# Decoder block on one core: sums of squares from a token-major input, phase tables made once and copied, GpSimd's wide work on VectorE

## The chip, the core and the metric

The kernel runs on one core of a Trainium2 chip. The core has five engines with a queue of instructions each, which run in order and meet by semaphores: TensorE (PE, matmuls; its weight loads are shown as PEld), VectorE (DVE), ScalarE (ACT), GpSimd (POOL) and SyncE (SP), which here only issues DMAs. The metric is the device time of one execution in microseconds. The comparison is with the median of three runs of the kernel before.

## What is computed

The reference is one decoder block on x of 1024 tokens by 1024 channels, in float32. After a normalization by the mean square of each token, one projection gives q, k, v, a gate and u. Retention of four heads takes q, k, v; a diagonal state-space model (S5) with 32 groups of 16 channels and 64 complex states takes u. Both results go through w_out, and a squared-ReLU MLP follows.

```python
h = rmsnorm(x, norm_mix_pre[i])                  # x * rsqrt(mean(x*x) + eps) * gain
q, k, v, gate, u = split(h @ w_in[i])
y_ret = silu(gate) * groupnorm(retention(rope(q), rope(k) * d**-0.5, v))
# S5: states s[l] = lam_bar * s[l-1] + b_bar u[l];  y = Re(c s) + d u
y_ssm = gelu(s5_scan(u, ...));  a, b = split(y_ssm @ w_glu[i]);  y_ssm = a * sigmoid(b)
x = x + rmsnorm(concat(y_ret, y_ssm) @ w_out[i])
h = rmsnorm(x, norm_mlp_pre[i])
x = x + rmsnorm(square(relu(h @ w_ff1[i])) @ w_ff2[i])
```

## The kernel before

Every float32 matmul operand is split in a high and a low part (split, ACT makes hi, DVE makes lo), and a product is three matmuls of 128x512 (mm3). Channels lie on the partitions; a tile is mostly 128x512, half of the tokens (hf 0 or 1). The order of instructions on each engine is made by the tile framework, which schedules with a timeline simulation; the code gives a sequence and a few extra dependences (load with a lead, in_place).

The front, up to the first matmul of w_out (tile mx), is what the change touches.

- x_half (L183) loads one of 16 halves of x, splits it, squares it in place on ACT (L190) and adds the square to xacc on POOL (L191). norm_sums turns xacc to sums per token with small matmuls (tile ns_x), rstd (L216) takes the power -1/2 on POOL (L220), norm_bcast spreads the result over the partitions with matmuls (tile nb_x), and ACT copies it to R (L277).
- The u product (L264 to L282) takes four PSUM banks for each half, u_0 and u_1. ACT evicts them to us (L273), DVE multiplies by R to uT (L280), and SP writes uT to DRAM (ud), from which the S5 parts read it back in another layout (UT).
- Between these, DVE makes the tables of S5: powers pw, qw, and vw, and the phase factors fa (16 steps) and fb (8 steps), by doubling (double_up, cmul).
- ssm_part runs for eight parts of four groups. outer makes W and VV (DVE, with one product, tmp, on POOL at L453); W gives kps and the Toeplitz tile MR (memset on POOL, eight DMAs), wps and WT. cmul at L490 makes the part's phase tables Fr and Fi, Fr on DVE and Fi on POOL (L310 to L312). xps = WT x UT; A and B are xps turned by Fr and Fi (L494 to L497, the last on POOL); a scan on DVE (L500); the turn back to SS (L503 on POOL, L505 to L509 on DVE); yps takes MR and SS; ACT applies the Gelu to Y, SP writes it to DRAM (yd), from which it comes back as ysT for the glu product.
- ssm() makes the parts run one behind the other, and tick() (L632) takes one step of them for each half of a gate or q/k projection (gate_unit, tile pg; qk_unit, tile pj), and two steps at every fourth tick. v_pair (tile v) comes after eight units. qk_unit applies rope on DVE and adds on POOL (L661). head_half is the retention; it multiplies q by xis on POOL (L600).
- After the projections come glu (tile gl), w_out (mx) and the MLP (f1, f2).

All loads and copies go through load (L114), on SP's queue. cmul (L306) writes one complex product as six operations, the first three on one engine and the last three on another, here V and GP for the phase tables:

```python
def cmul(e1, e2, o_r, o_i, ar, ai, br, bi, tr, ti):
    e1.tensor_tensor(o_r, ar, br, op=MUL)     # L307
    e1.tensor_tensor(tr, ai, bi, op=MUL)
    e1.tensor_tensor(o_r, o_r, tr, op=SUB)
    e2.tensor_tensor(o_i, ar, bi, op=MUL)     # L310
    e2.tensor_tensor(ti, ai, br, op=MUL)
    e2.tensor_tensor(o_i, o_i, ti, op=ADD)
```

Of the kernel before, what the change touches and what calls it, by code (L numbers as in the profile page):

```python
# [24 lines left out]
P = 128  # L25
D = 1024
L = 1024
KB = D // P
T = 8
NCH = L // P  # L30
H = 4
G = 32
# [18 lines left out]
def hybrid_block_kernel(ctx, tc, x, gain, wu, wv, wqkg, wglu, wout, wff1, wff2, lam, bc, dsk,  # L51
# [129 lines left out]
    hT, wus, xacc = [], [], [half("xacc0"), half("xacc1")]  # L181

    def x_half(k, hf):  # L183
        xr = half(f"x_{k}{hf}")
        load(xr, x[k][:, hs[hf]])
        r = split_new(f"h{k}{hf}", xr, g_pre[:, k:k + 1])
        if k == 0:
            S.activation(xacc[hf], xr, AF.Square)
        else:
            S.activation(xr, xr, AF.Square)  # L190
            GP.tensor_tensor(xacc[hf], xacc[hf], xr, op=ADD)  # L191
        return r

    for k in range(KB):
# [3 lines left out]
        hT.append([h0])  # L198
    for k in range(KB):
        hT[k].append(x_half(k, 1))  # L200
    lm = const("lm", [P, 3, G])
    load(lm, lam)
    sg_ = const("sgn_t", [P, 2])
    load(sg_, sgn)
    s_pm, s_mp = sg_[:, 0:1], sg_[:, 1:2]
# [8 lines left out]

# [49 lines left out]
    for hf in range(2):  # L264
# [9 lines left out]
        rr = norm_sums(f"x{hf}", [xacc[hf]], 4)  # L274
# [107 lines left out]
    def double_up(r, i, j, w, n):  # L382

        sh = [P, n, G]
        cmul(V, V, r[:, w:w + n], i[:, w:w + n], r[:, 0:n], i[:, 0:n],
             r[:, w - 1:w].to_broadcast(sh), i[:, w - 1:w].to_broadcast(sh),
             t8[:, 0, 0:n], t8[:, 1, 0:n])
# [17 lines left out]
    fa_r, fa_i = half("fa_r", shape=(P, 16, G)), half("fa_i", shape=(P, 16, G))  # L405
    fb = half("fb", shape=(P, 2, T, G))
# [5 lines left out]
    tt(fa_r[:, 0], t0, t1, MUL)  # L412
    tt(t0, sn, t1, MUL)
    ts(fa_i[:, 0], t0, s_mp, MUL)
    for w in (1, 2, 4, 8):
        double_up(fa_r, fa_i, 1, w, w)
# [3 lines left out]
    V.tensor_copy(fbr[:, 1], fa_r[:, 15])  # L420
    V.tensor_copy(fbi[:, 1], fa_i[:, 15])
    for w, n in ((1, 1), (2, 2), (4, 2)):
        double_up(fbr[:, 1:], fbi[:, 1:], 1, w, n)
    double_up(fbr[:, 1:], fbi[:, 1:], 1, 6, 1)
# [9 lines left out]

    def ssm_part(ei):
        g0 = ei * 4
# [6 lines left out]
        def outer(dst, a, lr, b, li, nm):  # L443
# [9 lines left out]
            GP.tensor_tensor(tmp, bx(b), by(li), op=MUL)  # L453
# [23 lines left out]
        Fr, Fi = half(f"Fr{ei}", shape=s3), half(f"Fi{ei}", shape=s3)  # L477
        A, B = half(f"A{ei}", shape=s3), half(f"B{ei}", shape=s3)
        shf = [P, 4, T, 16]

        def lowp(m):
            return m[:, :, gs].rearrange("p a g -> p g a").unsqueeze(2).to_broadcast(shf)

        def highp(m):
# [748 lines left out]
```

## Time and profile before

| | |
|---|---|
| time, median of 3 runs | 1126.47 us (1126.09 to 1129.38) |
| the profiled execution | 1127.15 us, span 1125.4 us |
| PE busy | 1065.6 us (95%) |
| DVE busy | 808.4 us (72%), 1433 instructions |
| ACT busy | 487.6 us (43%) |
| POOL busy | 218.9 us (19%), 149 instructions |
| first mx matmul | 401.81 us after the span's start |

Busy shares are means over the whole span. The page also cuts the span in 40 slices of 28 us and gives for each engine a digit, the busy tenths of the slice; so a stretch in which an engine is full stands out. Times in the rows below are from the start of the span. A duration of an instruction reaches from its start to its end with its latency; instructions of one engine overlap a little, so the distance from start to start is what one costs in a full queue.

### The profile page before, as it was taken

The numbers are of one execution on the slowest core, as the hardware profiler recorded it, in microseconds if no ns is written. First come the engines' busy times: TensorE is split into PE (matmuls) and PEld (weight loads), VectorE is DVE, ScalarE is ACT, GpSimd is POOL, SyncE is SP. The second block draws the span as 40 slices with busy tenths as digits, with TensorE's granted clock in tenths as the row PEclk, the third lists the DMA queues.
The fourth block names the chain that finished last, engine by engine and source line by source line (L and its number), as shares of the span: only waits on it lengthen the run. The fifth ranks groups of instructions, "written<-read, shape, count | busy, mean of one in ns | idle before, by whom it ended". The sixth has DMA issues, their size and how long they took to land.

```text
span 1125.4 us, 15280 instructions
## 1 busy us (share of the span) xinstructions
PE 1065.6 (95%) x5264; PEld 903.5 (80%) x5264; DVE 808.4 (72%) x1433; ACT 487.6 (43%) x900; POOL 218.9 (19%) x149
## 2 busy tenths in 40 slices
PE   7789796799999999999999999999999999999995
PEld 6577675698898888878888888888888888888895
DVE  7998989949654610657887788888575786675965
ACT  6411222332554522446665554456462445434712
POOL 4556676526311202230000000000000000000002
PEclk9898898899999999999999999999999999999998
DMA  8223122221123020438637667656793465569424
GB/s 297 79 53 104 49 82 87 60 72 62 34 95 103 20 75 1 168 127 306 222 116 240 225 224 235 231 195 228 281 371 99 156 207 184 171 225 349 137 69 156
DMA packets 122061, 174.24 MB, mean 155 GB/s; under 512 B 34944, under 2 KB 43136, under 8 KB 121984
## 3 DMA queue, kind: packets, MB, share of 16 engines
q1 hardware_dynamic: 121440, 172.75, 45.9%
q8 instruction: 41, 0.67, 0.2%
q10 hardware_dynamic: 544, 0.52, 0.1%
q14 instruction: 36, 0.29, 0.1%
HBM read 126.43 MB, written 45.61 MB: 153 GB/s over the span
## 4 chain that ended last, share of the span: by engine, by line
PE 78%; DVE 12%; issue 3%; SPq 2%; POOL 1%; DMA 1%; ACT 0%; DVEq 0%; ACTq 0%; POOLq 0%
PE f2x L106 15%; PE f2y L106 12%; PE f1z L106 8%; PE f1y L106 8%; PE mx L106 8%; PE f1x L106 7%; PE pj L106 4%; PE v L106 4%; PE gl L106 4%; PE f1w L106 4%; SPq L115 2%; DVE small L298 1%; DVE lo_wqkg L136 1%; DVE B L500 1%; DVE Fr L307 1%
## 5 line engine op out<-in xcount | busy, mean ns | idle before, releaser
L220 POOL TENSOR_TENSOR small<-small 128x4 f32<-128x4 f32 (+1 forms) x9 | 10.2, 1131 | 627.8 <-DVE small L218 627.8
L106 PE MATMUL f2x<-hi_tc,lo_sb 128*128 128x512 f32 x216 | 84.0, 389 | 0.0
L106 PE MATMUL f2x<-lo_tc,hi_sb 128*128 128x512 f32 x216 | 84.0, 389 | 0.0
L106 PE MATMUL f2x<-hi_tc,hi_sb 128*128 128x512 f32 x216 | 83.7, 390 | 0.0
L135 ACT ACTIVATE hi_sa<-rawa 128x512 fp32r<-128x512 f32 x80 | 48.3, 622 | 61.5 <-DVE rawa L799 57.2
L106 PE MATMUL f2y<-hi_tc,hi_sb 128*128 128x512 f32 x192 | 74.7, 389 | 0.0
L106 PE MATMUL f2y<-lo_tc,hi_sb 128*128 128x512 f32 x192 | 74.7, 389 | 0.0
L106 PE MATMUL f2y<-hi_tc,lo_sb 128*128 128x512 f32 x192 | 74.7, 389 | 0.0
L136 DVE TENSOR_TENSOR lo_sa<-rawa,hi_sa 128x512 fp32r<-128x512 f32 x80 | 56.1, 707 | 9.5 <-ACT hi_sa L135 9.5
L106 PE MATMUL pj<-hi_h,hi_wqkg 128*128 128x512 f32 x128 | 51.5, 402 | 0.0
L106 PE MATMUL pj<-lo_h,hi_wqkg 128*128 128x512 f32 x128 | 51.2, 400 | 0.0
L106 PE MATMUL pj<-hi_h,lo_wqkg 128*128 128x512 f32 x128 | 51.0, 399 | 0.0
L106 PE MATMUL f1x<-lo_tb,hi_sa 128*128 128x512 f32 x128 | 50.0, 390 | 0.3 <-DVE lo_tb L136 0.3
L106 PE MATMUL f1x<-hi_tb,hi_sa 128*128 128x512 f32 x128 | 50.1, 392 | 0.0
L106 PE MATMUL f1y<-hi_tb,hi_sa 128*128 128x512 f32 x128 | 49.8, 389 | 0.0
L106 PE MATMUL f1y<-lo_tb,hi_sa 128*128 128x512 f32 x128 | 49.8, 389 | 0.0
L106 PE MATMUL f1y<-hi_tb,lo_sa 128*128 128x512 f32 x128 | 49.8, 389 | 0.0
L106 PE MATMUL f1z<-hi_tb,hi_sa 128*128 128x512 f32 x128 | 49.8, 389 | 0.0
L106 PE MATMUL f1z<-lo_tb,hi_sa 128*128 128x512 f32 x128 | 49.8, 389 | 0.0
L106 PE MATMUL f1z<-hi_tb,lo_sa 128*128 128x512 f32 x128 | 49.8, 389 | 0.0
L106 PE MATMUL f1x<-hi_tb,lo_sa 128*128 128x512 f32 x128 | 49.3, 390 | 0.0
L106 PEld LDWEIGHTS f2x<-hi_tc,lo_sb 128*128 128x128 f32 x216 | 40.6, 188 | 8.5
(401 smaller groups left out, 3207.2 us busy)
## 6 DMA issues: line engine op xcount, KB each, us to landing
rawa<-wff_dram SPq DMA_DIRECT2D x92, 256.0 KB, 3.2
tinx<-td SPq DMA_DIRECT2D x48, 256.0 KB, 3.9
tiny<-td SPq DMA_DIRECT2D x48, 256.0 KB, 3.4
raw_wqkg<-wqkg_dram SPq DMA_DIRECT2D x24, 256.0 KB, 2.8
x<-x_dram SPq DMA_DIRECT2D x16, 256.0 KB, 5.1
raw_wo<-wout_dram SPq DMA_DIRECT2D x16, 256.0 KB, 4.1
xr<-x_dram SPq DMA_DIRECT2D x16, 256.0 KB, 4.1
xs<-mxs SPq DMA_DIRECT2D x16, 256.0 KB, 4.3
```

Source lines behind the costliest of these rows:

```text
L106: r = TE.matmul(out_, lhsT, rhs, **kw)
L115: r = nc.sync.dma_start(dst, src)
L135: after_mark(S.activation(hi, src, AF.Copy))
L136: V.tensor_tensor(lo, src, hi.bitcast(F32), op=SUB)
L220: GP.tensor_tensor(r, t, mhalf[:, 0:n], op=ALU.pow)
L298: V.scalar_tensor_tensor(o, a, s, b, op0=op0, op1=op1)
L307: e1.tensor_tensor(o_r, ar, br, op=MUL)
L500: V.tensor_tensor_scan(B[:, g], rho[:, g0 + g:g0 + g + 1].to_broadcast([P, P]), A[:, g], 0.0, op0=MUL, op1=ADD)
```

## The change

- The squares for the norm no longer come from the halves of x. A second copy of the input, xrow, with tokens on the partitions, is loaded in 16 pieces of 128x512 (x_sums), and ACT squares each with a running sum into a column of xsum. DVE adds two columns (new L278). xacc, its POOL additions and the ns_x matmuls are gone.
- fa and fb are half as wide: the partitions 0 to 63 hold the even parts' groups, 64 to 127 the odd ones'. They are doubled on POOL instead of DVE.
- phase_tables makes Fr and Fi for two parts in one pass (all six operations on DVE). Three DMAs for each of them spread them: the upper half to both halves of the odd part's tile, the lower half to the upper half of the even part's.
- The sign that the tables carried between halves is now in two scalar_tensor_tensor operations (new L525, L535).
- Every other wide operation of POOL in the front goes to DVE: tmp, A (twice), ra/rb, xis, rope.
- tick() takes one step each time.

```diff
@@ -178,31 +178,35 @@
     make_identity(nc, ident)
 
 
-    hT, wus, xacc = [], [], [half("xacc0"), half("xacc1")]
+    hT, wus = [], []
+    xsum = const("xsum", [P, 2, NCH])
 
     def x_half(k, hf):
         xr = half(f"x_{k}{hf}")
         load(xr, x[k][:, hs[hf]])
-        r = split_new(f"h{k}{hf}", xr, g_pre[:, k:k + 1])
-        if k == 0:
-            S.activation(xacc[hf], xr, AF.Square)
-        else:
-            S.activation(xr, xr, AF.Square)
-            GP.tensor_tensor(xacc[hf], xacc[hf], xr, op=ADD)
-        return r
-
+        return split_new(f"h{k}{hf}", xr, g_pre[:, k:k + 1])
+
+    def x_sums(hf):
+        for c in range(4 * hf, 4 * hf + 4):
+            for i in range(2):
+                xt = half(f"xt{c}{i}")
+                load(xt, xrow[c][:, hs[i]])
+                S.activation(xt, xt, AF.Square, accum_out=xsum[:, i, c:c + 1])
+
+    lm = const("lm", [P, 3, G])
+    load(lm, lam)
+    sg_ = const("sgn_t", [P, 2])
+    load(sg_, sgn)
+    s_pm, s_mp = sg_[:, 0:1], sg_[:, 1:2]
     for k in range(KB):
         h0 = x_half(k, 0)
         if k % 2 == 0:
             wus += wload(f"wu{k}", wu[k // 2])
         hT.append([h0])
+    x_sums(0)
     for k in range(KB):
         hT[k].append(x_half(k, 1))
-    lm = const("lm", [P, 3, G])
-    load(lm, lam)
-    sg_ = const("sgn_t", [P, 2])
-    load(sg_, sgn)
-    s_pm, s_mp = sg_[:, 0:1], sg_[:, 1:2]
+    x_sums(1)
     ed = const("ed", [GC, GC])
     load(ed, edge)
     dk = const("dk", [GC, G])
@@ -271,7 +274,9 @@
         us = [half(f"us_{hf}{b}") for b in range(4)]
         for b in range(4):
             S.activation(us[b], pss[b], AF.Copy)
-        rr = norm_sums(f"x{hf}", [xacc[hf]], 4)
+        sums = xsum[:, 0, 4 * hf:4 * hf + 4]
+        V.tensor_tensor(sums, sums, xsum[:, 1, 4 * hf:4 * hf + 4], op=ADD)
+        rr = rstd(f"x{hf}", sums, 4)
         rv.append(rr)
         R.append(half(f"R{hf}"))
         S.activation(R[hf], norm_bcast(f"x{hf}", rr, 4), AF.Copy)
@@ -379,12 +384,13 @@
     tt(t1, t1, t2, SUB)
     tt(ki, t1, t0, MUL)
 
-    def double_up(r, i, j, w, n):
-
-        sh = [P, n, G]
-        cmul(V, V, r[:, w:w + n], i[:, w:w + n], r[:, 0:n], i[:, 0:n],
+    def double_up(r, i, j, w, n, e=V):
+
+        sh = [P, n, r.shape[2]]
+        c = r.shape[2]
+        cmul(e, e, r[:, w:w + n], i[:, w:w + n], r[:, 0:n], i[:, 0:n],
              r[:, w - 1:w].to_broadcast(sh), i[:, w - 1:w].to_broadcast(sh),
-             t8[:, 0, 0:n], t8[:, 1, 0:n])
+             t8[:, 0, 0:n, 0:c], t8[:, 1, 0:n, 0:c])
 
     for w in (1, 2, 4):
         double_up(pr, pi, 1, w, w)
@@ -402,26 +408,33 @@
     ts(rho, e, 1.0, ADD)
 
 
-    fa_r, fa_i = half("fa_r", shape=(P, 16, G)), half("fa_i", shape=(P, 16, G))
-    fb = half("fb", shape=(P, 2, T, G))
+    G2 = G // 2
+    fa = half("fa", shape=(P, 2, 16, G2))
+    fa_r, fa_i = fa[:, 0], fa[:, 1]
+    fb = half("fb", shape=(P, 2, T, G))[:, :, :, 0:G2]
     ts(t0, cm, 1.0, ADD)
     tt(t1, t0, t0, MUL)
     tt(t2, sn, sn, MUL)
     tt(t1, t1, t2, ADD)
     ts(t1, t1, -0.5, MUL, 1.5, ADD)
-    tt(fa_r[:, 0], t0, t1, MUL)
-    tt(t0, sn, t1, MUL)
-    ts(fa_i[:, 0], t0, s_mp, MUL)
+    for i in range(2):
+        ph = slice(64 * i, 64 * i + 64)
+
+        def of_half(m):
+            return m[ph].rearrange("p (j i g) -> p j i g", i=2, g=4)[:, :, i]
+
+        for o, z in ((fa_r, t0), (fa_i, sn)):
+            tt(o[ph, 0].rearrange("p (j g) -> p j g", g=4), of_half(z), of_half(t1), MUL)
     for w in (1, 2, 4, 8):
-        double_up(fa_r, fa_i, 1, w, w)
+        double_up(fa_r, fa_i, 1, w, w, GP)
     fbr, fbi = fb[:, 0], fb[:, 1]
     V.memset(fbr[:, 0], 1.0)
     V.memset(fbi[:, 0], 0.0)
-    V.tensor_copy(fbr[:, 1], fa_r[:, 15])
-    V.tensor_copy(fbi[:, 1], fa_i[:, 15])
+    GP.tensor_scalar(fbr[:, 1], fa_r[:, 15], 1.0, None, op0=MUL)
+    GP.tensor_scalar(fbi[:, 1], fa_i[:, 15], 1.0, None, op0=MUL)
     for w, n in ((1, 1), (2, 2), (4, 2)):
-        double_up(fbr[:, 1:], fbi[:, 1:], 1, w, n)
-    double_up(fbr[:, 1:], fbi[:, 1:], 1, 6, 1)
+        double_up(fbr[:, 1:], fbi[:, 1:], 1, w, n, GP)
+    double_up(fbr[:, 1:], fbi[:, 1:], 1, 6, 1, GP)
     cs = half("cs", shape=(P, G, GC))
     ts(cs, a_c, s_pm, MUL)
     de = half("de", shape=(P, G, GC))
@@ -432,7 +445,35 @@
     s3 = (P, 4, P)
     s4 = (P, 4, T, GC)
 
+    phases = {}
+
+    def phase_tables(j):
+
+        gs = slice(4 * j, 4 * j + 4)
+        shf = [P, 4, T, 16]
+
+        def lowp(m):
+            return m[:, :, gs].rearrange("p a g -> p g a").unsqueeze(2).to_broadcast(shf)
+
+        def highp(m):
+            return m[:, :, gs].rearrange("p a g -> p g a").unsqueeze(3).to_broadcast(shf)
+
+        def v4(m):
+            return m.rearrange("p g (b a) -> p g b a", a=16)
+
+        even, odd = ([half(f"F{z}{2 * j + i}", shape=s3) for z in "ri"] for i in range(2))
+        tr, ti = half(f"ftr{j}", shape=s3), half(f"fti{j}", shape=s3)
+        cmul(V, V, v4(even[0]), v4(even[1]), lowp(fa_r), lowp(fa_i), highp(fbr), highp(fbi),
+             v4(tr), v4(ti))
+        for e, o in zip(even, odd):
+            load(o[0:64], e[64:128])
+            load(o[64:128], e[64:128])
+            load(e[64:128], e[0:64])
+        phases[2 * j], phases[2 * j + 1] = even, odd
+
     def ssm_part(ei):
+        if ei % 2 == 0:
+            phase_tables(ei // 2)
         g0 = ei * 4
         gs = slice(g0, g0 + 4)
         UT = half(f"UT{ei}", shape=s3)
@@ -450,7 +491,7 @@
             V.tensor_tensor(dst, bx(a), by(lr), op=MUL)
-            GP.tensor_tensor(tmp, bx(b), by(li), op=MUL)
+            V.tensor_tensor(tmp, bx(b), by(li), op=MUL)
             V.tensor_tensor(dst, dst, tmp, op=ADD)
@@ -474,36 +515,25 @@
         VV = half(f"VV{ei}", shape=s4)
         outer(VV, a_c, vr, b_c, vi, "v")
         yield
-        Fr, Fi = half(f"Fr{ei}", shape=s3), half(f"Fi{ei}", shape=s3)
+        Fr, Fi = phases.pop(ei)
         A, B = half(f"A{ei}", shape=s3), half(f"B{ei}", shape=s3)
-        shf = [P, 4, T, 16]
-
-        def lowp(m):
-            return m[:, :, gs].rearrange("p a g -> p g a").unsqueeze(2).to_broadcast(shf)
-
-        def highp(m):
-            return m[:, :, gs].rearrange("p a g -> p g a").unsqueeze(3).to_broadcast(shf)
-
-        def v4(m):
-            return m.rearrange("p g (b a) -> p g b a", a=16)
-
-        cmul(V, GP, v4(Fr), v4(Fi), lowp(fa_r), lowp(fa_i), highp(fbr), highp(fbi), v4(A), v4(B))
         xps = mi_ps(f"xps{ei}", s3)
         for g in range(4):
             TE.matmul(xps[:, g], WT[:, g], UT[:, g], start=True, stop=True)
         V.tensor_tensor(A, xps, Fr, op=MUL)
         V.tensor_tensor(B[0:64], xps[64:128], Fi[64:128], op=MUL)
-        V.tensor_tensor(B[64:128], xps[0:64], Fi[0:64], op=MUL)
-        GP.tensor_tensor(A, A, B, op=ADD)
+        V.scalar_tensor_tensor(B[64:128], xps[0:64], -1.0, Fi[0:64], op0=MUL, op1=MUL)
+        V.tensor_tensor(A, A, B, op=ADD)
         yield
         for g in range(4):
             V.tensor_tensor_scan(B[:, g], rho[:, g0 + g:g0 + g + 1].to_broadcast([P, P]),
                                  A[:, g], 0.0, op0=MUL, op1=ADD)
         n1 = P - 1
-        GP.tensor_tensor(A[:, :, 0:n1], B[:, :, 0:n1], Fr[:, :, 0:n1], op=MUL)
+        V.tensor_tensor(A[:, :, 0:n1], B[:, :, 0:n1], Fr[:, :, 0:n1], op=MUL)
         C = half(f"C{ei}", shape=s3)
         V.tensor_tensor(C[0:64, :, 0:n1], B[64:128, :, 0:n1], Fi[64:128, :, 0:n1], op=MUL)
-        V.tensor_tensor(C[64:128, :, 0:n1], B[0:64, :, 0:n1], Fi[0:64, :, 0:n1], op=MUL)
+        V.scalar_tensor_tensor(C[64:128, :, 0:n1], B[0:64, :, 0:n1], -1.0, Fi[0:64, :, 0:n1],
+                               op0=MUL, op1=MUL)
         SS = half(f"SS{ei}", shape=s3)
         V.memset(SS[:, :, 0], 0.0)
         V.tensor_tensor(SS[:, :, 1:P], A[:, :, 0:n1], C[:, :, 0:n1], op=SUB)
@@ -556,7 +586,7 @@
             load(t, rope[:, i, hs[hf]], 20.0)
-            GP.tensor_tensor(t, t, R[hf], op=MUL)
+            V.tensor_tensor(t, t, R[hf], op=MUL)
             pair.append(t)
@@ -597,7 +627,7 @@
                                        sps[:, i], op0=MUL, op1=ADD)
-        GP.tensor_tensor(q_, q_, xis[:, h].unsqueeze(1).to_broadcast(list(s3)), op=MUL)
+        V.tensor_tensor(q_, q_, xis[:, h].unsqueeze(1).to_broadcast(list(s3)), op=MUL)
         yield
@@ -631,7 +661,7 @@
         ticks[0] += 1
-        step(2 if ticks[0] % 4 == 0 else 1)
+        step(1)
         pstep(1)
@@ -658,7 +688,7 @@
             V.tensor_tensor(b, b, tabs[1][hf], op=MUL)
-            GP.tensor_tensor(af, af, b, op=ADD)
+            V.tensor_tensor(af, af, b, op=ADD)
             pair.append(a)
```

Three places in the order of instructions. On POOL before, from the second R on, the first S5 parts (MR: the Toeplitz tile; B and Fi: the phase table; A: the turned xps):

```order
L465 MEMSET MR_1021 128x512
L311 TENSOR_TENSOR B_929<-fa_i,fb 128x512
L310 TENSOR_TENSOR Fi_927<-fa_r,fb 128x512
L453 TENSOR_TENSOR tmpw_1211<-bc_261,qw 128x512
L312 TENSOR_TENSOR Fi_927<-Fi_927,B_929 128x512
L497 TENSOR_TENSOR A_928<-A_928,B_929 128x512
L503 TENSOR_TENSOR A_928<-B_929,Fr_926 128x4x127
```

On POOL now, from the power for the first R on:

```order
L223 TENSOR_TENSOR small<-small 128x4
L312 TENSOR_TENSOR fa<-fa 128x16
L313 TENSOR_TENSOR t_610<-fa 128x16
L315 TENSOR_TENSOR fa<-fa 128x16
L316 TENSOR_TENSOR t_610<-fa 128x16
L314 TENSOR_TENSOR fa<-fa,t_610 128x16
L317 TENSOR_TENSOR fa<-fa,t_610 128x16
L312 TENSOR_TENSOR fa<-fa 128x32
```

The wide products are gone; 50 small ones, of 16 to 128 columns, stand between the powers for the first and the second R, and beside powers only memsets of MR follow in the front.

On ACT before, around the eviction of the second u product (us_10 to us_13), which frees the banks for the gate projections:

```order
L277 ACTIVATE R0_386<-nb_x0_387 128x512
L273 ACTIVATE us_10_505<-u_1_0_405 128x512
L273 ACTIVATE us_11_506<-u_1_1_406 128x512
L273 ACTIVATE us_12_507<-u_1_2_407 128x512
L273 ACTIVATE us_13_508<-u_1_3_408 128x512
L462 ACTIVATE small_72<-kps0_782 128x64
```

On ACT now, behind us_10, the square of xt51 and us_11:

```order
L194 ACTIVATE xt60_262,small_72<-xt60_262 128x512
L194 ACTIVATE xt61_265,small_72<-xt61_265 128x512
L541 ACTIVATE MT0_1004<-MR0_815 128x8x4x16
L503 ACTIVATE small_72<-kps1_881 128x64
L276 ACTIVATE us_12_519<-u_1_2_419 128x512
L514 ACTIVATE WT1_898<-wps1_899 128x512
L674 ACTIVATE gb00_863<-ga00_862 128x512
L194 ACTIVATE xt70_268,small_72<-xt70_268 128x512
L135 ACTIVATE hi_wqkg8_0_942<-raw_wqkg8_0_940 128x512
L194 ACTIVATE xt71_271,small_72<-xt71_271 128x512
L135 ACTIVATE hi_wqkg8_1_948<-raw_wqkg8_1_946 128x512
L276 ACTIVATE us_13_520<-u_1_3_420 128x512
```

The four evictions that stood together now have five squares of token-major pieces and the copies of the first S5 parts between them.

On SP before, the copies of the first parts (ud: u to DRAM; MR: the Toeplitz tile):

```order
L115 DMA ud<-uT_399 128x8x64
L115 DMA ud<-uT_402 128x8x64
L115 DMA MR_789<-small 128x64
L115 DMA MR_789<-small 112x64
L115 DMA MR_789<-small 96x64
L115 DMA MR_789<-small 80x64
```

On SP now, from the third write of u on:

```order
L115 DMA ud_284<-uT_02_411 128x8x64
L115 DMA Fr1_778<-Fr0_776 64x512 x2
L115 DMA Fi1_779<-Fi0_777 64x512 x2
L115 DMA xt71_271<-xrow_dram 128x512
L115 DMA MR1_888<-small_72 128x64
L115 DMA Fr0_776<-Fr0_776 64x512
L115 DMA Fi0_777<-Fi0_777 64x512
```

The table copies stand ahead of the last token-major piece, xt71; the last two wait for the two copies ahead of them to land, since they overwrite what those read.

## Rows read from the trace of the kernel before

**Rows 1.** The page: busy time, and DVE's busy tenths in 40 slices.

```profile
PE 1065.6 (95%) x5264; PEld 903.5 (80%) x5264; DVE 808.4 (72%) x1433; ACT 487.6 (43%) x900; POOL 218.9 (19%) x149
...
DVE  7998989949654610657887788888575786675965
```

**Rows 2.** Windows: stretch, its length, engines' busy us (instructions), granted clock, DMA.

```profile
31.06:42.20 11.14, 2.88 (x7) 2.31 (x8) 11.04 (x20) 8.59 (x16) 7.75 (x6) 0.65 0.14 48
...
168.37:182.20 13.83, 4.39 (x24) 4.35 (x24) 13.69 (x16) 3.65 (x8) 9.34 (x6) 0.63 0.15 46
...
228.28:401.97 173.69, 173.66 (x1122) 157.22 (x1121) 104.71 (x229) 77.68 (x160) 49.23 (x33) 1.00 0.23 73
```

**Rows 3.** Waits of PE, 0 to 402 us: us in total, times, longest.

```profile
PE yps L515 <- DVE SS L509: 26.5, 5, 9.4
PE u L106 <- ACT us L273: 8.3, 1, 8.3
```

**Rows 4.** Timeline near 24.6 us, DVE and POOL: start, duration, instruction.

```profile
24.68 1.28 DVE L290 TENSOR_SCALAR small<-small 128x32 f32<-128x32 f32 x1
...
24.61 1.31 POOL L191 TENSOR_TENSOR xacc<-xacc,x 128x512 f32<-128x512 f32 x1 [1.36 <-ACT x L190]
```

**Rows 5.** The line L509: duration in ns, shortest, median and longest of eight.

```profile
L509 DVE TENSOR_TENSOR SS<-A,C x8: 667/1525/1855, 113.9 to 284.3; 128x508 f32<-128x508 f32 x8
```

**Rows 6.** Windows, columns as in rows 2: part 0's A to part 5's SS.

```profile
102.50:223.40 120.90, 94.97 (x476) 80.36 (x475) 112.65 (x147) 32.88 (x57) 75.89 (x48) 0.89 0.26 75
```

**Rows 7.** POOL's groups, 0 to 402 us: busy us, mean ns, idle before them.

```profile
L191 POOL TENSOR_TENSOR xacc<-xacc,x 128x512 f32<-128x512 f32 x14 | 21.1, 1504 | 17.6 <-ACT x L190 17.0
...
L614 POOL TENSOR_TENSOR small<-small 128x4 f32<-128x4 f32 x8 | 10.1, 1268 | 30.7 <-DVE small L613 28.1 <-ACT hi_wglu L135 2.6
...
masks.py:199 POOL TENSOR_SCALAR_AFFINE_SELECT small<-small 128x128 f32<-128x128 f32 x1 | 0.3, 292 | 0.0
...
L1223 POOL MEMSET const-float32-1.0<- 128x1 f32 x1 | 0.1, 98 | 0.0
```

**Rows 8.** Timelines of DVE and of POOL, 71 to 95 us.

```profile
71.28 0.18 DVE L307 TENSOR_TENSOR fa_r<-fa_r 128x32 f32<-128x32 f32 x1
...
78.31 0.41 DVE L312 TENSOR_TENSOR fa_i<-fa_i,t 128x256 f32<-128x256 f32 x1
...
89.09 0.67 DVE L454 TENSOR_TENSOR W<-W,tmpw 128x512 f32<-128x512 f32 x1
89.69 0.67 DVE L645 SCALAR_TENSOR_TENSOR ga<-gb,ga 128x512 f32<-128x512 f32 x1
...
86.45 7.89 POOL L311 TENSOR_TENSOR B<-fa_i,fb 128x512 f32<-128x512 f32 x1 [2.37 <-DVE small L463]
```

**Rows 9.** Timeline of PE at six places; brackets: idle before, and what ended it.

```profile
27.84 0.39 PE L106 MATMUL u<-hi_h,lo_wu 128*128 128x512 f32 x1
28.07 0.39 PE L106 MATMUL u<-hi_h,hi_wu 128*128 128x512 f32 x1
...
39.32 0.80 PE L106 MATMUL u<-hi_h,hi_wu 128*128 128x512 f32 x1 [8.26 <-ACT us L273]
...
96.13 1.22 PE L493 MATMUL xps<-UT,WT 128*128 128x128 f32 x4 [2.37 <-DMA UT<-ud]
...
106.80 1.05 PE L493 MATMUL xps<-UT,WT 128*128 128x128 f32 x8
...
401.81 0.39 PE L106 MATMUL mx<-hi_r,hi_wo 128*128 128x512 f32 x1
```

**Rows 10.** The chain of waits from 228 us: start, duration, engine and line.

```profile
228.28 23.39 PE v L106 x192
```

**Rows 11.** SP's timeline, 105 to 115 us: start, time to issue, DMAs.

```profile
105.40 4.99 SPq L115 DMA_DIRECT2D MR<-small  x8
...
111.05 3.72 SPq L115 DMA_DIRECT2D UT<-ud  x8
```

**Rows 12.** The page's DMA issues: count, size, median us to landing.

```profile
x<-x_dram SPq DMA_DIRECT2D x16, 256.0 KB, 5.1
```

More of the change, by code (lines that the diff above doesn't have):

```diff
@@ L50, in hybrid_block_kernel @@
 @with_exitstack
-def hybrid_block_kernel(ctx, tc, x, gain, wu, wv, wqkg, wglu, wout, wff1, wff2, lam, bc, dsk,
+def hybrid_block_kernel(ctx, tc, x, xrow, gain, wu, wv, wqkg, wglu, wout, wff1, wff2, lam, bc, dsk,
                         rope, dmask, xi, zeta, sgn, edge, out):
@@ L1209, in _arrays @@
     dsk = cont(np.asarray(ssm_d)[0].reshape(G, GC).T)
-    return [xT, gain, wu, wv, wqkg, wglu, wout, wff1, wff2, lam, bc, dsk] + _constants()
-NAMES = ("x", "gain", "wu", "wv", "wqkg", "wglu", "wout", "wff1", "wff2", "lam", "bc", "dsk",
+    xrow = cont(np.asarray(x)[0].reshape(NCH, P, D))
+    return [xT, xrow, gain, wu, wv, wqkg, wglu, wout, wff1, wff2, lam, bc, dsk] + _constants()
+NAMES = ("x", "xrow", "gain", "wu", "wv", "wqkg", "wglu", "wout", "wff1", "wff2", "lam", "bc", "dsk",
          "rope", "dmask", "xi", "zeta", "sgn", "edge")
```

## The prediction

> **What bounds the kernel now.** I read the page first: TensorE (PE) is busy 95% of the span, and VectorE (DVE) is full only in the first nine of forty slices [rows 1]. So the time is PE's work plus what PE loses in the front, and the loss has to be looked for before 230 us. The chain of waits says the same: from the first v matmul at 228.28 on it is PE nearly without a break [rows 10], and up to the first mx matmul PE is busy 173.66 of 173.69 us at full clock [rows 2].
>
> The loss is PE's time less its own work. Own work is a count of the matmuls in the order, each at its spacing at full clock: 0.227 us for 512 columns, 0.11 for 128 [rows 9], 0.122 for v's 256 columns (23.39 us by 192) [rows 10]. This gives 155.9 us up to the first v and 328.5 up to the first mx, which starts at 401.81 [rows 9]. PE loses 72.4 us before 228.28, some 6 of them before the first weights are there. Two other places show the kind: at 31.06 the second u product waits 8.26 us for the eviction of the first [rows 3, 9]; yps waits five times, 26.5 us in all, for SS, the last DVE result of an SSM part [rows 3]. Each is followed by half clock: in 31.06:42.20 and 168.37:182.20 the granted clock is 0.65 and 0.63 of 2.4 GHz [rows 2].
>
> Why is DVE late? One form, SS (L509), takes 0.667 us at its shortest and 1.855 at its longest [rows 5]. The long ones stand beside GpSimd (POOL): a 128x32 DVE operation that starts at 24.68, inside POOL's xacc addition of 24.61 to 25.92, takes 1.28 us [rows 4], the same width alone 0.18 [rows 8]. Priced start to start (0.60 us for 128x512: 89.09 to 89.69 [rows 8]), the DVE instructions from part 0's A to part 5's SS are 83 us of work. They took 120.9, of which 112.65 is shown as busy [rows 6]. POOL ran 48 instructions there, 43 of them wide (the others are MR memsets). So 38 us are lost to 43 wide POOL operations, 0.88 each.
>
> **The change part by part.** Everything up to the first mx changes; PE's order behind it is the same, so I carry the difference at the first mx to the end of the profiled execution, 1127.15 us (the median of the runs is 0.7 less).
>
> *Removed.* 98 wide POOL operations. At 0.88 each that is 86 us of DVE time in the stretch up to mx, but only where DVE sets the pace. Eight ns_x matmuls go, under 1 us.
>
> *Moved to DVE.* 60 of the 98 (16 tmp, 16 A, 16 ra/rb, 8 xis, 4 rope) at 0.60 to 0.62 is 37 us. The phase tables are six wide operations for two parts instead of three for each, so DVE's share stays. The doubling of fa and fb leaves DVE (48 small operations, some 10 us). DVE's own work up to the first mx rises from 248 to 277 us. Between A of part 0 and SS of part 4 it is now 141 instructions, 80 us: seven at 1.0, 25 at 0.7, 81 at 0.6 and 28 small ones.
>
> *Moved to POOL.* A chain of 50 small dependent operations, with no rival for its results: Fr of part 0 waits for its end. The trace has no such operation. From below, a 128x1 memset is 0.10 us, so 5 us; from above, a 128x4 pow is 1.27 in the mean [rows 7], so 63 us, and beside a packed DVE one wide POOL operation took 7.89 us [rows 8]. I take 0.3, from the 128x128 select at 0.29 [rows 7] and DVE's own prices of 0.18 to 0.41 for this arithmetic [rows 8]: 15 us. DVE waits for R0 while most of the chain runs, so contention is small.
> This is a place where the Trainium skill speaks against the change: GPSIMD Engine Reference, section 4.1 Engine selection, puts two-input elementwise work on VectorE and calls GpSimd about 2x slower. An estimate by that page, twice the 10 us these cost on DVE, is a 20 us chain and a time 5 us above mine; no row here shows a pair of one width on both engines undisturbed.
>
> *Sums of squares.* ACT's squares no longer wait for DVE's lo_h, and the us evictions no longer stand behind them: the 8.26 us [rows 9] fall to some 1.5, with most of the half clock. But 16 loads of 256 KB come on SP's queue, with three buffers. Five of the squares stand between the us_1 evictions on ACT, and their loads stand on SP behind ud, MR and the copies of Fr0/Fi0, which wait for DVE's tables, which wait for POOL's chain. An input load takes 5.1 us to land in the median [rows 12], under full DMA load; I take 3 here.
>
> *The walk.* x lands as before. fa's seed on DVE comes at about 48 (19 us of DVE's own work after the last lo_h, at 29) instead of just before 71.28 [rows 8], because 21 wide POOL operations (14 xacc, 5 tmp, 2 rope) are gone before it. POOL's chain runs to 63, all of u on PE to 54, R0 comes at 55. Fr0 and Fi0 are ready at 69, xt71 lands at 72, us_13 at 75, pg20 at 81, nb_x1 82.5, R1 84, uT_10 and its way through ud and UT 93.5. xps0, which now stands behind 83.6 us of PE work instead of 66.6, runs at 98; it ran at 96.13 [rows 9]. So the front half gains 15 us: 29.5 were lost before it, now 14.4.
>
> *The parts.* From xps0 to yps of part 4 PE has 79.6 us of work and DVE 80: nearly equal, in a ring (WT, xps, A, SS, yps). I allow 10 us for the two waiting on each other and 3 for the half clock. From v on PE has 25 us without need of DVE and the cover returns. Where an SSM step now comes once a tick (step(1)), part 7's yps stands at 257 to 266 us of PE work, right before glu at 267; before there were 46 us between them. Its way through yd and ysT, about 8 us against 8 of PE's own: I put 2.
>
> *Sum.* 98 + 244.6 (PE's own work from xps0 to mx) + 10 + 3 + 2 = 357.6 for the first mx, against 401.8. That is 44 us less: 1127.15 - 44.2 = 1083. What is late next is SP.
>
> **The rivals.**
> *PE sets the pace.* Nothing waits from u on: 6.2 + 328.2 + 5 of remaining half clock = 340, a gain of 62: 1065. For it: 86 us of contention go where 72 were lost. Against: the ring above, DVE as full as PE.
>
> *SP sets the pace.* Per part SP issues eight MR copies (4.99 us), eight UT (3.72) [rows 11], eight ysT (about as UT), yd, three weight loads and three table copies at about 0.5: 16 us, five parts 80, as long as PE. The table copies wait for each other's landing (2 to 3 us), and everything behind them on SP, xt71 and later MR and UT with it. At 3 us of such waiting a part, 15 us more than I allow: 1098. The token-major loads late by 10 us would give 1093 in the same way. For it: all 24 copies and 16 loads go into the one queue that already issues for some 14 us a part.
>
> *POOL's chain is dear.* Each us beyond 15 delays Fr0, xt71, us_13, R1 and xps0 one for one. At 1.02 us an operation the chain is 51: 1083 + 36 = 1119; at 0.5, 1093.
>
> *Slower: the moved work is all that counts.* If the long DVE operations are only recorded as long, or POOL's work beside DVE is worth what it replaced, DVE's own 277 us instead of 248 come to the front: 1127 + 29 = 1156. The point is 29 us by 98 removed operations: below 0.30 us each the change loses. The stretch shows 0.88, and one form at 0.667 and 1.855 [rows 5], so it gets little. Perfetto Trace Analysis of the Trainium skill, section Optimizing Scalar/DVE Operations, says that a saturated DVE may be relieved by GpSimd, and adds that with a shared read port it might not help; the rows bear out the second half.
>
> **How the numbers follow.** The forecast (1070 to 1090) gets 0.45, PE's pace (1055 to 1070) 0.15, SP's (1090 to 1105) 0.20, the dear chain (1090 to 1119) 0.12, gains and losses that cancel within 0.3% 0.03, the moved work alone 0.05. The time is the first one's, 1083. The range leaves out the slower cases and the end of the dear chain: 1060 to 1108. A measurement of this kernel can tell 0.3% from no change: faster 0.92, same 0.03, slower 0.05.
>
> **What would show it.** First mx near 358. SS near 0.67 at every place; no DVE operation over 1.2 us between 100 and 200 us. The gap at 31 us under 2 us. POOL's chain from about 48 to 63. xps0 near 98. What would make it wrong: SP's queue waiting for the landing of table copies with UT behind it; R0 or us_13 late on ACT behind a square whose data are not there; a glu matmul that waits for ysT.

## The result and the profile after

The changed kernel takes 1077.43 us in the median (1077.2 to 1078.13, four runs) against 1126.43 for the kernel before: a ratio of 0.9561, 95% interval 0.9544 to 0.9577. That is 49 us less. The forecast was 1083, the range 1060 to 1108.

The page of the kernel after, for [rows 1]: POOL has given up two thirds of its busy time, DVE has more instructions and less busy time, and PE is full or nearly so from the second slice on.

```profile
PE 1049.9 (98%) x5248; PEld 891.5 (83%) x5248; DVE 770.1 (72%) x1446; ACT 492.6 (46%) x916; POOL 68.8 (6%) x101
...
PE   7998999999999999999999999999999999999995
```

Windows of the kernel after, columns as in [rows 2]: the stretch of the old gap at 31 us, the stretch of [rows 6], the time from the first xps to the last wait for SS, and from there to the first mx.

```profile
31.06:42.20 11.14, 11.14 (x51) 9.23 (x50) 11.14 (x55) 3.08 (x9) 0.00 (x0) 1.00 0.70 233
...
102.50:223.40 120.90, 119.53 (x738) 106.65 (x738) 104.86 (x186) 45.29 (x83) 2.63 (x5) 1.00 0.35 96
...
101.20:182.32 81.12, 81.12 (x483) 71.57 (x481) 78.95 (x140) 29.97 (x53) 2.11 (x4) 1.00 0.38 106
...
184.00:351.84 167.84, 167.70 (x1080) 151.32 (x1079) 115.65 (x265) 79.67 (x157) 11.31 (x9) 1.00 0.29 86
```

In 102.50 to 223.40 PE is busy 119.53 us instead of 94.97 [rows 6], at full clock instead of 0.89. In the third row PE and DVE are both full; that row bears on the last experiments.

All waits of PE up to 360 us, for [rows 3], and the line of SS, for [rows 5] (L509 is L539 now). yps waited 26.5 us and now waits 1.4; SS is at its shortest everywhere.

```profile
PE u L106 <- ACT hi_h L138: 5.9, 1, 5.9
PE nb_x L247 <- POOL small L223: 5.8, 1, 5.8
PE yps L545 <- DVE SS L539: 1.4, 1, 1.4
```

```profile
L539 DVE TENSOR_TENSOR SS<-A,C x8: 666/680/687, 111.6 to 288.7; 128x508 f32<-128x508 f32 x8
```

The timeline of PE, for [rows 9]: the broadcast of the second norm, the first xps, the last wait for SS, the first mx.

```profile
84.57 2.07 PE L247 MATMUL nb_x<-small 128*128 128x128 f32 x8 [5.77 <-POOL small L223]
...
101.87 1.05 PE L522 MATMUL xps<-UT,WT 128*128 128x128 f32 x8
...
183.69 0.49 PE L545 MATMUL yps<-SS,VV 128*128 128x128 f32 x2 [1.37 <-DVE SS L539]
...
351.84 0.39 PE L106 MATMUL mx<-hi_r,hi_wo 128*128 128x512 f32 x1
```

The first mx comes 50.0 us sooner than in [rows 9], and from there to the end of the span both kernels take 723.6 us. So the whole gain lies ahead of mx. Against PE's own work (328.5 us before, 328.2 after, by the same count) it lost 73.3 us and now loses 23.6. Gaps of over 1 us before mx were 45.8 us in all and are 13.0; half clock ruled for 51 us and now for 6.8 (some of it lies in the gaps, so the two do not add).

### The profile page after: what moved, and what is told of

Its sections match the earlier page's. It is cut to its first block, busy times and chain, and to the rows that moved or that the text cites. A ratio compares the mean times of both kernels' runs of the same rounds, so it can differ in the third digit from the quotient of the medians.

```text
span 1075.5 us, 15286 instructions
## 1 busy us (share of the span) xinstructions
PE 1049.9 (98%) x5248; PEld 891.5 (83%) x5248; DVE 770.1 (72%) x1446; ACT 492.6 (46%) x916; POOL 68.8 (6%) x101
## 4 chain that ended last, share of the span: by engine, by line
PE 79%; DVE 2%; issue 1%; DMA 1%; POOL 1%; ACT 1%; DVEq 0%; SPq 0%; ACTq 0%; POOLq 0%
PE f2x L106 15%; PE f2y L106 12%; PE f1z L106 8%; PE f1y L106 8%; PE mx L106 8%; PE f1x L106 8%; PE pj L106 4%; PE gl L106 4%; PE f1w L106 4%; PE v L106 3%; PE y L636 1%; PE st L611 1%; DMA raw_wo<-wout_dram 1%; PE y L638 1%; PE sps L622 1%
## 5 line engine op out<-in xcount | busy, mean ns | idle before, releaser
L106 PEld LDWEIGHTS f2x<-lo_tc,hi_sb 128*128 128x128 f32 x216 | 40.6, 188 | 8.4
```

What stands on the lines that cost most here:

```text
L106: r = TE.matmul(out_, lhsT, rhs, **kw)
```

## Experiments

Each kernel was timed beside the kernel before on its chip, so ratios to it are compared; the changed kernel's is 0.9561. A difference of 0.001 is 1.1 us; the intervals are about 0.0015 to each side.

### One part at a time

e5: the kernel before with every wide POOL operation of the front on DVE, and nothing else (98 operations; Fi stays as its own table, xacc stays).

```diff
-            GP.tensor_tensor(xacc[hf], xacc[hf], xr, op=ADD)
+            V.tensor_tensor(xacc[hf], xacc[hf], xr, op=ADD)
...
-        cmul(V, GP, v4(Fr), v4(Fi), lowp(fa_r), ...
+        cmul(V, V, v4(Fr), v4(Fi), lowp(fa_r), ...
```

> The kernel before with all 98 wide GpSimd operations of the front moved to VectorE (xacc and Fi too) and nothing else: no second input, tables as before, fa and fb on VectorE, ticks as before. VectorE's own work up to the first mx rises by 60 us (248 to 308); from A of part 0 to SS of part 5 it is 107 us against the 121 that the stretch took before. Theory (0.88 us of VectorE's time lost per wide GpSimd operation, 0.6 to 1.0 gained back by doing it there): 10 to 17 us less, 1110 to 1117 us; the moved work nearly eats what it frees. Rival (more work on the fullest engine is slower): 1140 us or more.

Measured: 1093.72 us, ratio 0.9707 (0.9686 to 0.9727). Both sizes were wrong: moving alone gives 33 us, two thirds of the whole. DVE got 98 operations more, 59 us of work at the 0.60 of [rows 8], and the kernel became 33 us faster. The page of e5, the line of SS and the wait of u for us:

```profile
PE 1055.4 (97%) x5264; PEld 895.5 (82%) x5264; DVE 805.9 (74%) x1531; ACT 488.5 (45%) x900; POOL 53.0 (5%) x51
```

```profile
L509 DVE TENSOR_TENSOR SS<-A,C x8: 669/678/682, 107.9 to 257.4; 128x508 f32<-128x508 f32 x8
```

```profile
PE u L106 <- ACT us L273: 0.4, 1, 0.4
```

DVE's busy time is 805.9 us against 808.4 [rows 1], with 98 instructions more: what the moved work costs it gets back from its other instructions. The wait of u for us, 8.3 us before, is 0.4 here, though the squares are where they were; so moving the POOL work takes this wait away by itself, as the new sums do in e6. The prediction had put it down to the squares' place alone.

e6 is the kernel before with the token-major sums alone (x_sums, the loads, two columns added on DVE), e7 with the tables alone (fa and fb half as wide, doubled on POOL, phase_tables with its copies, the signs), e8 the changed kernel with the old sums.

> The kernel before with only the sums of squares changed (token-major input, ScalarE with a running sum, no xacc, no ns_x). Theory (the front half wins its 8 us wait at 31 us with the half clock behind it and 14 GpSimd operations, but the S5 parts stay at VectorE's pace of 22 us): 8 to 14 us less, 1113 to 1119 us. Rival (the front is where the gain comes from): 1080 to 1100 us.

> The kernel before with only the phase tables changed: fa and fb half as wide on GpSimd, Fr and Fi for two parts in one pass on VectorE, spread by 24 DMAs; Fi is off GpSimd (24 wide operations fewer), the other wide work stays there. From A of part 0 to SS of part 5 VectorE's own work is 80 us and 27 wide GpSimd operations remain: 80 + 27 x 0.88 = 104 against 121. Theory: 10 to 17 us less, 1110 to 1117 us. Rival (the copies in SP's queue and GpSimd's chain behind its wide work cost what the tables save): 1126 us or more.

> The changed kernel with only the sums of squares as before (squares in place on ScalarE, xacc on GpSimd, ns_x matmuls, no second input). Theory: 14 xacc operations of 0.88 us and the first eviction behind the squares come back, but five token-major squares no longer stand between the us_1 evictions: 3 to 13 us more, 1080 to 1090 us. Rival (the token-major loads in SP's queue cost as much as they free): 1072 to 1079 us.

Measured: e6 1119.51 us (ratio 0.993), e7 1112.67 (0.9869), e8 1093.35 (0.9697). e7 lies in its expected range, e6 0.5 us above it and e8 3 us above. The parts alone give 7.5, 14.3 and 33.0 us, 55 together against 49. They overlap: the 14 xacc operations leave POOL in e5 and in e6, the 24 of Fi in e5 and in e7. Beside the others the sums are worth 15 us (e8), alone half of that. PE's waits up to mx tell why; of e6, with the sums alone:

```profile
PE yps L521 <- DVE SS L515: 28.6, 6, 9.5
PE kps L467 <- DVE W L460: 8.5, 1, 8.5
```

The wait of u for us (8.3 us [rows 3]) is gone as foreseen, but W on DVE is not ready, and kps waits as long as u had waited; yps waits as before, since the wide POOL work is still there. In e7 u waits 8.7 us and yps 18.0. I read from this that an early front is worth something only when DVE can keep up.

### What a POOL operation costs DVE

e1 adds to the changed kernel, in five of the parts, eight POOL additions that read VV and write a tile that nobody uses; e2 adds twenty memsets of that tile instead, behind one small addition for the same place in the order. Neither takes anything from the computation.

```diff
         outer(VV, a_c, vr, b_c, vi, "v")
+        if 2 <= ei <= 6:
+            for _ in range(8):          # e2: range(20), GP.memset(junk, 0.0)
+                GP.tensor_tensor(junk, VV, VV, op=ADD)
```

> The changed kernel with 40 additions of 128x512 on GpSimd that read the tile VV of the S5 parts 2 to 6 (eight each) and write a tile that nobody reads; nothing waits for them. Theory (a wide GpSimd operation that reads SBUF holds up VectorE): 24 of the 40 (parts 2 to 4) fall where VectorE sets TensorE's pace; at the 0.88 us each that the kernel before lost, 21 us more, 1093 to 1100 us, and long VectorE operations of 1.2 to 2 us come back in the trace. Rival (GpSimd's work costs VectorE nothing, the gain came from elsewhere): 1077 to 1079 us, SS stays at 0.68 us.

> The control to the run with reads: at the same places 20 memsets of 128x512 for each of the parts 2 to 6 instead of eight additions, so about the same time on GpSimd (20 x 0.53 us against 8 x 1.3), the same delay to the MR memsets behind them, but no SBUF reads. Theory (the reads are what VectorE meets): 1077 to 1080 us and no long VectorE operations. Rival (any busy GpSimd holds VectorE up, or the queue behind the extra work is what costs): the same loss as with the additions, 1093 us or more.

Measured: e1 1103.36 us, ratio 0.9777 (0.9763 to 0.9792), 3 us above the theory's range; e2 1080.36, 0.9574 (0.9558 to 0.959). Forty additions cost 24 us; a hundred memsets cost 1.5, the size of the interval. From A of part 0 to SS of part 4 DVE takes 102.75 us with the reads and 79.50 with the writes. The window of each, then forms of DVE and POOL's added work in 102 to 206 us (count, busy us, mean ns); first e1:

```profile
102.25:205.00 102.75, 87.38 (x466) 76.07 (x465) 102.07 (x139) 29.61 (x54) 47.90 (x36) 0.91 0.30 81
...
L520 POOL TENSOR_TENSOR junk<-VV 128x512 f32<-128x512 f32 x32 | 46.0, 1436 | 27.7 <-DVE VV L496 25.5
...
L533 DVE TENSOR_TENSOR_SCAN B<-small,A 128x128 f32<-128x128 f32 x20 | 13.4, 726 | 0.0
L694 DVE TENSOR_TENSOR rb<-rb,rope 128x512 f32<-128x512 f32 x8 | 6.7, 839 | 0.1
...
L691 DVE TENSOR_TENSOR ra<-pj,rope 128x512 f32<-128x512 f32 x8 | 5.5, 683 | 0.1
```

And e2:

```profile
103.30:182.80 79.50, 78.13 (x460) 68.57 (x459) 78.82 (x140) 29.46 (x54) 39.33 (x76) 1.00 0.38 105
...
L521 POOL MEMSET junk<- 128x512 f32 x100 | 52.7, 527 | 5.6
...
L534 DVE TENSOR_TENSOR_SCAN B<-small,A 128x128 f32<-128x128 f32 x20 | 6.9, 400 | 0.0
...
L695 DVE TENSOR_TENSOR rb<-rb,rope 128x512 f32<-128x512 f32 x8 | 5.5, 686 | 0.1
```

The same DVE work (139 and 140 instructions) is busy 102.07 and 78.82 us. So 32 additions cost it 23.3 us, 0.73 each; each is itself shown at 1.44. The theory had counted 24 in this stretch; it became longer, part 5's eight fell into it, and that accounts for the greater loss.

The means hide two kinds of instances, so single rows are needed. e1, DVE and then POOL, and all 32 scans (shortest, median and longest ns):

```profile
174.07 0.69 DVE L691 TENSOR_TENSOR ra<-pj,rope 128x512 f32<-128x512 f32 x1
...
175.41 1.52 DVE L495 TENSOR_TENSOR tmpv<-bc,vw 128x512 f32<-128x512 f32 x1
...
180.70 0.67 DVE L695 TENSOR_TENSOR ra<-ra,rb 128x512 f32<-128x512 f32 x1
...
179.57 5.44 POOL L520 TENSOR_TENSOR junk<-VV 128x512 f32<-128x512 f32 x1
```

```profile
L533 DVE TENSOR_TENSOR_SCAN B<-small,A x32: 386/402/1258, 105.6 to 309.5; 128x128 f32<-128x128 f32 x32
```

In 102 to 206 us the eight scans beside an addition take about 1.2 us and the other twelve 0.4; tmpv takes 1.52 beside one. ra at 174.07, which lies wholly beside an addition, takes its usual 0.69: it reads one operand from PSUM (pj, the result of a matmul), the longer ones both from SBUF, where all other tiles lie. The kernel before shows the same more broadly. Four of its forms that read PSUM (A and the first B from xps, ga, ra) run 40 times before mx, 20 of them for over 0.5 us beside a wide two-input POOL operation, and none takes over 0.694 us. Two of the forms:

```profile
L495 DVE TENSOR_TENSOR B<-xps,Fi x8: 692/693/693, 103.2 to 275.7; 64x512 f32<-64x512 f32 x8
```

```profile
L657 DVE TENSOR_TENSOR ra<-pj,rope x16: 660/676/692, 156.2 to 317.3; 128x512 f32<-128x512 f32 x16
```

In e2, 65 DVE operations stand for over 0.5 us beside a memset, and the forms that the additions lengthened keep 0.66 to 0.69 us there, the tables' products 1.04 to 1.07. The Trainium skill has this rule (SBUF — State Buffer, section Who interferes with whom): a DVE instruction with two SBUF inputs is held up by a GpSimd instruction that reads SBUF, not by one that only writes it, and one with at most one SBUF input, outside DVE's two-port modes, is not held up. These rows agree with both halves of it. A single input in SBUF is not always enough: the TENSOR_SCALAR of [rows 4], with one input tile there, took 1.28 us beside an addition, and no run here shows in which mode it ran.

POOL can be the one that waits, too. The addition at 179.57 takes 5.44 us, while the seven DVE operations that start between 180.10 and 184.04 run close together at their usual times.

e3 puts 60 of the wide operations back on POOL (tmp, both products of A, ra/rb, xis, rope), in the changed kernel.

```diff
-            V.tensor_tensor(tmp, bx(b), by(li), op=MUL)
+            GP.tensor_tensor(tmp, bx(b), by(li), op=MUL)
...
-        V.tensor_tensor(A, A, B, op=ADD)
+        GP.tensor_tensor(A, A, B, op=ADD)
```

> The changed kernel with the 60 moved operations (tmp, A twice, ra, xis, rope) back on GpSimd; sums of squares, tables and step(1) stay changed. VectorE's own work from A of part 0 to SS of part 4 falls from 80 to 63 us, and 27 wide GpSimd operations come into this stretch. Theory: 27 x 0.88 = 24 us of loss against 17 us of relief, and GpSimd becomes a link in the chain of each part: 1085 to 1095 us. Rival (moving this work is not what gained, or even cost): 1060 to 1077 us.

Measured: 1097.84 us, ratio 0.9732 (0.9715 to 0.9748), 19 us more than the changed kernel and, like e1, somewhat more than expected. If an operation costs DVE p when it is on POOL and 0.61 when DVE does it, 60 x (p - 0.61) = 19 gives p = 0.93; the same sum for e5, 98 x (p - 0.60) = 33, gives 0.94. The prediction had 0.88. These sums are end to end: they also hold the time in which DVE waits for POOL's results (in e3 4.5 us for tmpw and 2.3 for A) and PE's lost clock. PE waits 10.8 us for SS again, in four places.

### The chain on POOL

e4: the changed kernel with the doubling of fa and fb on DVE.

```diff
-        double_up(fa_r, fa_i, 1, w, w, GP)
+        double_up(fa_r, fa_i, 1, w, w)
```

> The changed kernel with the doubling of fa and fb back on VectorE (half as wide, 50 operations of about 0.1 to 0.2 us start to start, 6 us in all) instead of GpSimd's chain of 15.7 us. VectorE stands idle 5.3 us for R0 and 4.1 us for the chain there. Theory (the chain's time delays the first tables and with them the second half of u): the tables come some 6 us sooner and the first mx 3 to 6 us, 1071 to 1075 us. Rival (VectorE's own work sets the front): 6 us more, 1083 us.

Measured: 1083.68 us, ratio 0.9606 (0.959 to 0.9622): 5 us slower than with the chain on POOL, the rival's number. Part 0's A comes 5 us sooner (97.8 for 103.0), but SS of part 4 only one (181.9 for 182.9), and PE waits 7.6 us for SS instead of 1.4. What the early start gives is spent on DVE before part 4 is through.

### What bounds the changed kernel

e9 restores the rule of two steps at every fourth tick. e10 and e11 give the token-major pieces 4 and 6 buffers instead of 3, so that their squares on ACT no longer stand between the us_1 evictions and the second R comes sooner. e12 is e11 and e9 together.

```diff
-        step(1)
+        step(2 if ticks[0] % 4 == 0 else 1)     # e9, e12
...
-BUFS = {"x": 8, "rawwu": 8, ...
+BUFS = {"x": 8, "xt": 6, "rawwu": 8, ...        # e11, e12; 4 in e10
```

> The changed kernel with the old rule of tick() (two steps at every fourth tick). Theory (the first mx starts one stretch of PE's own work after the last SS that PE had to wait for; that was SS of part 4, 166.4 us before mx, at 183): with the old rule PE has 163.5 us of own work behind yps of part 4 and 154.9 behind that of part 5, and DVE's own work to these two SS ends at 161.6 and 170.6 us instead of being the last of a denser order; each us that SS of part 4 comes sooner or later is given back nearly in full, so the two orders differ by little: 1073 to 1081 us, same. Rival (one step a tick is what keeps yps of the last parts from being late, so the rule itself carries some of the gain): yps waits again at parts 5 to 7, 1085 to 1095 us, first mx behind 358. Rival on the other side (one step a tick puts yps of part 7 directly ahead of glu, and this costs): glu no longer waits, 1070 to 1073.

> The changed kernel with four buffers instead of three for the token-major pieces. Theory (what is left in the front is the late square of xt71, hence nb_x1, hence R1, uT of the second half and with it xps and all parts): the squares no longer stand behind the us_1 evictions on ACT, nb_x1 comes by PE's own count 23 us of work sooner, PE's 5.8 us wait for POOL's power before nb_x1 is gone, SS of part 4 comes some 6 to 10 us sooner, but PE has 173.6 us of own work behind it instead of 166.4: first mx at 342 to 349, 1068 to 1075 us. Rival (the front is bound by DVE's own work, which the earlier R1 doesn't shorten): same, 1075 to 1080. Rival (more token-major loads ahead of the last pieces of x hold up h7 and lo_h of the second half, and u waits): 1080 to 1090, with a new wait of PE for hi_h or lo_h between 30 and 55 us.

> The changed kernel with six buffers instead of three for the token-major pieces. Theory: as with four buffers, and since DVE's own work up to A of part 0 is shorter still (68.6 against 72.3 us) at the same PE work behind SS of part 4 (173.8 us): 1066 to 1074 us. Rival (more loads ahead of x): six loads of 256 KB instead of one or two stand ahead of the second half of x on SP, at some 1.5 us each by the loads' rate, so PE waits for hi_h of the second half, and the gain is gone: 1076 to 1088, worse than with four buffers.

> Six buffers for the token-major pieces and the old rule of tick() together. Theory: the gains of the two are those that they have alone, added, within 3 us (the front by the buffers, the parts by the rule): if six buffers give -6 and the old rule 0, 1068 to 1074. Rival: the parts' ring (xps, A, SS, yps) takes back what the front gave, since DVE is nearly full there in either order: 1075 to 1081.

Measured: e9 1079.79 us (0.9581, 0.9568 to 0.9594), e10 1079.56 (0.9578), e11 1078.58 (0.9567, 0.9554 to 0.958), e12 1078.21 (0.9565). None can be told from the changed kernel. e9 came as its theory said. For e10 and e11 the theory fell, and so did the rival of late x, though e11's time lies in its range: no wait for hi_h beyond the first is there. e10's other rival (same, 1075 to 1080) has the time right. e12 leaves both of its ideas standing: with e11 and e9 worth nothing alone, adding them up gives nothing either. The front did become earlier, by 25 us at the first xps, as e11's timeline, its waits of PE and the window from the first xps to SS of part 4 show:

```profile
77.03 1.13 PE L522 MATMUL xps<-UT,WT 128*128 128x128 f32 x8 [1.93 <-DMA UT<-ud]
...
352.37 0.39 PE L106 MATMUL mx<-hi_r,hi_wo 128*128 128x512 f32 x1
```

```profile
PE yps L545 <- DVE SS L539: 5.9, 4, 2.5
PE u L106 <- ACT hi_h L138: 5.5, 1, 5.5
PE xps L522 <- DMA UT<-ud: 1.9, 1, 1.9
```

```profile
77.00:175.90 98.90, 93.66 (x496) 79.77 (x496) 97.27 (x167) 32.93 (x58) 2.11 (x4) 0.98 0.41 111
```

The wait of 5.8 us for nb_x is gone, and 6.4 us came back: yps waits 4.5 us more and xps 1.9. The first mx is at 352.4 as before. In 101.20 to 182.32 of the changed kernel PE is busy all of 81.12 us and DVE 78.95 (third row of the windows above). In e11 DVE is busy 97.27 of the 98.90 us from the first xps to SS of part 4, and PE waits. My reading is that DVE has no room there for work that comes sooner, as e12's rival says (the ring takes back what the front gave); no run with six buffers and less work on DVE tests it.

## Why the prediction was right, and where its terms were off

**The mechanism held.** The time went where the prediction put it: long DVE instructions beside POOL, the wait of u for us, and the half clock behind both. The rival that the moved work alone counts (1156) falls by e5 and e3, where the same operation costs about 0.33 us more on POOL than on DVE, not less. The price of 0.88 held, but not as the time that DVE's instructions grow by. In the 120.9 us of [rows 6] DVE is busy 112.65, so 8.25 of the 38 us were idle, most of them waits for POOL's results:

```profile
DVE B L500 <- POOL A L497: 4.1, 4, 1.2
DVE B L495 <- POOL Fi L312: 1.9, 1, 1.9
```

By busy time alone the stretch gives (112.65 - 83) / 43 = 0.69, close to the 0.73 of e1, where nothing waits for POOL; the 0.93 and 0.94 of e3 and e5 are end to end.

**The walk held to 2 us until the second norm.** fa's seed came at 47.90 (48 foreseen), the chain ended at 64.20 (63), R0 came at 53.82 (55), the tables were ready at 70.7 (69), us_13 at 76.31 (75). Then nb_x1 came at 84.57 (82.5), R1 at 86.68 (84) and xps0 at 101.87 (98). The rows of the kernel after around that place, DVE and POOL:

```profile
81.34 1.00 DVE L316 TENSOR_TENSOR fti<-fa,fb 128x512 f32<-128x512 f32 x1
82.27 0.15 DVE L221 TENSOR_SCALAR small<-small 128x4 f32<-128x4 f32 x1
82.33 1.27 DVE L136 TENSOR_TENSOR lo_wqkg<-raw_wqkg,hi_wqkg 128x512 fp32r<-128x512 f32 x2
...
82.50 2.02 POOL L223 TENSOR_TENSOR small<-small 128x4 f32<-128x4 f32 x1 [14.88 <-DVE small L221]
```

The small operation L221 of the norm comes behind the tables of the next pair in DVE's order, three us after the sums that it needs (L278, at 79.14), and the power on POOL, 1.03 us for the first half, takes 2.02 beside two-input work on DVE. PE meanwhile stood 5.77 us, and the granted clock was 0.50 in 83.0 to 89.8, 6.8 us that begin in this wait. So the term "14.4 lost before xps0" was too small: 18.3 by the same count.

**The price of the chain was right, its pieces were not alike.** Fifty operations in 15.7 us are 0.31 each, for 0.3 taken. Rows of POOL after, by width, and the one that stood beside a wide DVE operation:

```profile
49.36 0.21 POOL L315 TENSOR_TENSOR fa<-fa 128x16 f32<-128x16 f32 x1
...
52.14 0.32 POOL L316 TENSOR_TENSOR t<-fa 128x64 f32<-128x64 f32 x1
...
54.19 0.46 POOL L316 TENSOR_TENSOR t<-fa 128x128 f32<-128x128 f32 x1
...
57.63 2.26 POOL L313 TENSOR_TENSOR t<-fb 128x16 f32<-128x16 f32 x1
```

Start to start, 128x64 and 128x128 cost POOL 0.27 and 0.42 us; DVE in the same kernel takes 0.14 and 0.20 for these widths (the powers pw, at 34 to 36 us). That agrees, operation by operation, with what the Trainium skill says in the place that the prediction cites (GPSIMD Engine Reference, section 4.1 Engine selection: about twice as slow). The whole chain took 15.7 us and not the 20 estimated by it; fa and fb are half as wide as the arrays behind the 10 us on DVE. And the place was right all the same, as e4 shows.

**The parts lost less than allowed.** 10 + 3 + 2 us were allowed from xps0 to mx; the stretch took 250.0 us against 244.6 of own work, so 5.4. The term that failed is the 10 for PE and DVE waiting on each other: yps waits 1.4 us in all. The lengths of both were right (PE 80.4 from the first xps to its wait for SS of part 4, 79.6 foreseen; DVE 79.9 from A of part 0 to this SS, 80 foreseen). The scheduler had laid the two orders side by side, and with DVE's instructions at their short durations they now run as laid. That this is why so little was lost is my reading; no experiment here isolates the scheduler. The glu wait (2) did not show.

**Sum.** 3.9 us too little before xps0 and 9.6 too much behind it: 357.6 foreseen, 351.84 measured, 1083 for 1077.4. The two errors cancel in part, so that the forecast came as close as 5.6 us is partly luck.

**The other rivals.** SP: the table copies land in 2.3 us in the median, as feared, but between 60 and 260 us SP stood only 2.0 us for them, and up to mx the waits of PE name no DMA. The dear chain falls by its 15.7 us. PE's pace (1065) is 12 us off, though PE does wait little. Of the 23.6 us that PE still loses before mx, 5.9 pass before the first operands are there, 5.8 are the wait for nb_x, 1.4 the wait for SS, at most 3.4 the half clock behind nb_x, and 2.4 the first twelve u matmuls, which start mostly 0.427 us apart instead of 0.227, after 5.88 us without work for PE. Rows of them and of the stretch in which the granted clock is 0.50:

```profile
7.75 1.91 PE L106 MATMUL u<-lo_h,hi_wu 128*128 128x512 f32 x4
9.45 1.91 PE L106 MATMUL u<-hi_h,lo_wu 128*128 128x512 f32 x4
...
87.72 0.63 PE L106 MATMUL pg<-lo_h,hi_wqkg 128*128 128x512 f32 x1
88.15 0.63 PE L106 MATMUL pg<-hi_h,lo_wqkg 128*128 128x512 f32 x1
```

The distance is the same, 0.427. The trace records the clock from 11.29 us on, and there the distance falls to 0.23; the 1.00 that a window shows before that is a missing record. So by their spacing the first twelve run at the lower of the clock's two levels, as the first ten do in the kernel before (its record begins at 10.53). The 4.7 left are spread over the matmuls; I did not settle on which.

**Signs.** SS at 666 to 687 ns, no idle PE in 31.06 to 42.20, and the chain in 48 to 64 came as listed; xps0 came 4 us late and the first mx 6 us early; the one-operation DVE times between 100 and 200 us end at 1.1 (the tables' products), where 23 stood above 1.2 before.

## What to carry over

Price an operation on POOL by what it does to DVE: here a wide operation that reads SBUF cost DVE 0.7 us of its own time and the kernel up to 0.94 where DVE also waited for its result, more than the 0.60 that DVE needs to do it itself. A hundred memsets cost 1.5 us, and a chain of small operations was 5 us cheaper on POOL than on DVE. When an early stage is made earlier, look first whether the stage behind it has an engine with room: 25 us at the first xps gave nothing, and DVE was busy 97.27 of the next 98.90 us. Parts of a change need not add up: the sums were worth 7.5 us alone and 15 in company.

## What was not expected of the hardware

That the delay depends on where DVE's operands are: beside an addition on POOL a scan went from 0.4 to 1.2 us, while forms with one operand in PSUM stayed under 0.70, in 20 instances of the kernel before. That memsets on POOL left DVE alone: of e2's hundred, of 527 ns each, 68 fell in the stretch from A of part 0 to SS of part 4, in which DVE was busy 78.82 of 79.50 us, against 79.25 of 79.90 without them. And that POOL can be the one that waits: one addition took 5.44 us, where most took 1.04 to 1.6, while DVE's operations stood close together.
